# All stores of a grouped softmax move to SyncE's DMA ring, in turn with the loads

## The chip, the cores and the metric

The kernel runs on one core of one Trainium2 chip. Its time is device microseconds for one execution. Before the change it took 1326.51 us, the median of 4 runs that lie between 1326.36 and 1326.7 us. One further execution was taken with the hardware profiler on; the profile below is of that one.

The engines that matter here are VectorE (DVE in the profile), ScalarE (ACT), GpSimd (POOL) and SyncE (SP). All transfers between the chip's main memory and the on-chip buffers are made by the core's 16 DMA engines. An instruction stream that issues a transfer (SyncE's or GpSimd's) only puts work into a ring of its own on each of those 16 engines. TensorE does nothing in this kernel.

## The reference

The input x has the shape (4, 4096, 4352) in float32. Each row of 4352 numbers is cut into 8 groups of 544, and every group gets its own softmax:

```python
x_g = x.reshape(B, N, 8, 544)
x_g = x_g - x_g.max(axis=-1, keepdims=True)
exp = np.exp(x_g)
out = exp / exp.sum(axis=-1, keepdims=True)
```

There are 16,384 rows. 285.2 MB are read and 285.2 MB are written, and each number is used in only a handful of operations.

## The kernel before

A tile is 256 rows: 128 partitions with two rows each, so 8704 numbers (34,816 bytes) in every partition and 4352 KB in all. There are 64 tiles (`nt`), numbered from 0, and six buffers of that size (`NT = 6`, `bufs`). Tile t lives in buffer t modulo 6, and everything is done in place there.

For each tile the work is as follows.

- **Load.** SyncE issues one transfer for the whole tile (line 105). Only the last tile, 63, is loaded as two halves of one row per partition (line 108), so that its computation can begin half a tile earlier. Completion is counted on the semaphore `landed` of that buffer.
- **Maximum.** VectorE makes the negated maximum of the 16 groups of each partition in one instruction (`vector_max`, line 62). It waits for `landed`.
- **Exponential.** ScalarE makes 16 instructions, one for each group, which add the negated maximum, take exp and leave the group's sum (`scalar_exp`, line 86).
- **Scaling.** VectorE takes the reciprocal of the 16 sums (line 72) and multiplies the tile by it (line 75), which raises the semaphore `scaled` by one (`vector_scale`).
- **Store.** Tiles 0 to 61 are stored by GpSimd (line 118), one transfer each, counted on the semaphore `stored` of the buffer. The last two tiles (`LAST = 2`) are stored by SyncE (line 113).

VectorE's own order is written out at the end of the kernel: the maximum of tile n+1 comes ahead of the scaling of tile n. So the scaling of tile n stands behind the landing of tile n+1.

Two queues are set by hand. SyncE's queue holds the 64 loads in order; before the load of tile t, from tile 6 on, it waits until `stored` says that tile t-6 has left the buffer (line 102). After the last load come the last two stores, each behind its wait on `scaled`. GpSimd's queue holds 62 stores, each behind its wait on `scaled` (line 117), and then the final waits for everything that was stored. The two queues fill two different rings on each of the 16 DMA engines: loads are in the one, stores in the other.

Of the kernel before, what the change touches and what calls it, by code (L numbers as in the profile page):

```python
# [1 line left out]

# [4 lines left out]


@with_exitstack
def kernel(  # L10
    ctx: ExitStack,
    tc: tile.TileContext,
    x: bass.AP,
    out: bass.AP,
):
    nc = tc.nc
    G = 8
    P = 128
    R = 2
    NT = 6  # L20
    RG = R * G
    xf = x.flatten_outer_dims()
    of = out.flatten_outer_dims()
    N, D = xf.shape
    Dg = D // G
    nt = N // (P * R)
    LAST = 2
    FIRST = 2
    turns = (nt - 1 - FIRST) // NT
    f32 = mybir.dt.float32  # L30
    X = mybir.AxisListType.X
    Exp = mybir.ActivationFunctionType.Exp
    xt = xf.rearrange("(t p r) d -> t p (r d)", p=P, r=R)
    ot = of.rearrange("(t p r) d -> t p (r d)", p=P, r=R)

    landed = [tc.alloc_semaphore(f"landed{b}") for b in range(NT)]
    stored = [tc.alloc_semaphore(f"stored{b}") for b in range(NT)]
    last_landed = tc.alloc_semaphore("last_landed")
    last_stored = tc.alloc_semaphore("last_stored")


    max_done = tc.alloc_semaphore("max_done")
    exp_done = tc.alloc_semaphore("exp_done")
    rec_done = tc.alloc_semaphore("rec_done")
    scaled = tc.alloc_semaphore("scaled")

    ctx.enter_context(tc.tile_critical(  # L47
        sync_engine=mybir.EngineType.Pool, no_gpsimd_drain=True))
    bufs = [ctx.enter_context(nc.sbuf_tensor(f"xt{b}", [P, R * D], f32)) for b in range(NT)]
    mx = ctx.enter_context(nc.sbuf_tensor("mx", [P, NT, RG], f32))  # L50
    sm = ctx.enter_context(nc.sbuf_tensor("sm", [P, NT, RG], f32))
    rs = ctx.enter_context(nc.sbuf_tensor("rs", [P, NT, RG], f32))

    parts = [(t, slice(0, RG)) for t in range(nt - 1)]
    parts += [(nt - 1, slice(r * G, (r + 1) * G)) for r in range(R)]

    def groups(t, g):
        return bufs[t % NT][:, :].rearrange("p (g d) -> p g d", d=Dg)[:, g, :]

    def vector_max(n):  # L60
        t, g = parts[n]
        i = nc.vector.reduce_max(  # L62
            out=mx[:, t % NT, g], in_=groups(t, g), axis=X, negate=True)
        if g.start == 0:
            i.wait_op(landed[t % NT], 16 * (t // NT + 1), "sem-ge")
        else:
            i.wait_op(last_landed, 16, "sem-ge")
        i.then_inc(max_done, 1)

    def vector_scale(n):  # L70
        t, g = parts[n]
        nc.vector.reciprocal(out=rs[:, t % NT, g], in_=sm[:, t % NT, g]).wait_op(  # L72
            exp_done, n + 1, "sem-ge").then_inc(rec_done, 1)
        xg = groups(t, g)
        nc.vector.tensor_tensor(  # L75
            out=xg,
            in0=xg,
            in1=rs[:, t % NT, g].unsqueeze(2).to_broadcast([P, g.stop - g.start, Dg]),
            op=mybir.AluOpType.mult,
        ).wait_op(rec_done, n + 1, "sem-ge").then_inc(scaled, 1)  # L80

    def scalar_exp(n, count):
        t, gs = parts[n]
        xg = groups(t, gs)
        for g in range(gs.start, gs.stop):
            i = nc.scalar.activation(  # L86
                out=xg[:, g - gs.start, :],
                in_=xg[:, g - gs.start, :],
                func=Exp,
                bias=mx[:, t % NT, g:g + 1],  # L90
                scale=1.0,
                accum_out=sm[:, t % NT, g:g + 1],
            )
            if g == gs.start:
                i.wait_op(max_done, count, "sem-ge")
        i.then_inc(exp_done, 1)

    for t in range(nt):  # L100
        if t >= NT:
            nc.sync.wait_ge(stored[t % NT], 16 * (t // NT))
        tile_in = bufs[t % NT]
        if t < nt - 1:
            nc.sync.dma_start(out=tile_in[:, :], in_=xt[t]).then_inc(landed[t % NT], 16)  # L105
        else:
            for r in range(R):
                nc.sync.dma_start(
                    out=tile_in[:, r * D:(r + 1) * D], in_=xt[t, :, r * D:(r + 1) * D],
                ).then_inc(landed[t % NT] if r < R - 1 else last_landed, 16)  # L110
    for t in range(nt - LAST, nt):
        nc.sync.wait_ge(scaled, t + 1 if t < nt - 1 else len(parts))
        nc.sync.dma_start(out=ot[t], in_=bufs[t % NT][:, :]).then_inc(last_stored, 16)


    for t in range(nt - LAST):
        nc.gpsimd.wait_ge(scaled, t + 1)
        nc.gpsimd.dma_start(out=ot[t], in_=bufs[t % NT][:, :]).then_inc(stored[t % NT], 16)  # L118
    for t in range(nt - NT, nt - LAST):
        nc.gpsimd.wait_ge(stored[t % NT], 16 * (t // NT + 1))  # L120
    nc.gpsimd.drain()
    nc.gpsimd.wait_ge(last_stored, 16 * LAST)

    nc.scalar.preload_act_table(Exp)  # L124

    for n in range(FIRST):
        scalar_exp(n, n + 1)
    nc.scalar.sem_inc(max_done, -FIRST)
    with nc.scalar.Fori(0, turns):
        for k in range(NT):  # L130
            scalar_exp(FIRST + k, k + 1)
        nc.scalar.sem_inc(max_done, -NT)
    for k, n in enumerate(range(FIRST + turns * NT, len(parts))):
        scalar_exp(n, k + 1)


    vector_max(0)
    for n in range(len(parts)):
        if n + 1 < len(parts):
            vector_max(n + 1)  # L140
        vector_scale(n)


# [1 line left out]
_INS = ['x']  # L145
_OUTS = [((4, 4096, 4352), 'float32')]


# [23 lines left out]
```

## Time and profile before

| what | before |
|---|---|
| median of 4 runs | 1326.51 us (1326.36 to 1326.7) |
| the profiled execution, its own time | 1326.34 us |
| the profiled execution, its span from first to last instruction | 1324.6 us |
| VectorE busy | 1190.0 us (90%) |
| ScalarE busy | 757.4 us (57%) |
| GpSimd busy | 33.3 us (3%) |
| moved by DMA | 570.48 MB, mean 431 GB/s |

The page's first part gives the busy time of each engine. Its second part cuts the span in 40 equal slices and gives, for each, the busy share of the engines and of the 16 DMA engines (a 9 is 90% or more) and the rate at which these moved bytes. The third part tells apart the rings by their kind: the hardware kind is the one that SyncE's transfers fill, the software kind the one that GpSimd's fill, and the small third one brings instructions. The fifth part lists the costliest groups of instructions, each with its line, its count, its busy time in all, the mean of one, and the idle time of the engine just before them with what ended it. The sixth part lists the transfers with the time from issue to landing.

Of the execution's 1326.34 us, 1.7 us lie outside the span.

### The profile page before, as it was taken

The page shows a single profiled execution, that of the slowest core. Times are in us where ns is not written, and L with a number is a line of the kernel's source. Part 1 is how long each engine was busy: PE and PEld are TensorE (multiplying, and loading weights), DVE is VectorE, ACT ScalarE, POOL GpSimd, SP SyncE. Part 2 cuts the span into 40 slices and gives each one's busy share as a digit, 9 for nine tenths or more (in the row PEclk, how much of TensorE's full clock was granted, in tenths as well). Part 3 has the DMA queues.
Part 4 walks back from the last instruction along what each step waited for, and adds up shares of the span by engine and source line. Part 5 has one row for each costly group of instructions (what it writes and reads, how often), then busy time and mean ns, then how long its engine had stood idle before and what let it go on. Part 6 is the DMA issues. An engine that isn't in the chain of part 4 may idle for free.

```text
span 1324.6 us, 2465 instructions
## 1 busy us (share of the span) xinstructions
DVE 1190.0 (90%) x195; ACT 757.4 (57%) x2049; POOL 33.3 (3%) x66
## 2 busy tenths in 40 slices
DVE  5999999988989889898898998988989889898893
ACT  3765566547456465564655646556465474654751
POOL 0000000000000000000000000000000000000000
DMA  9999999999999999999999999999999999999998
GB/s 404 421 433 437 430 432 434 436 432 430 436 432 435 431 434 432 435 431 434 432 437 428 435 433 435 430 434 433 435 434 430 433 435 435 429 436 433 434 429 374
DMA packets 18582, 570.48 MB, mean 431 GB/s; under 512 B 2064, under 2 KB 2064, under 8 KB 2064
## 3 DMA queue, kind: packets, MB, share of 16 engines
q1 hardware_dynamic: 9648, 294.13, 51.5%
q0 software_dynamic: 8928, 276.30, 48.3%
q14 instruction: 6, 0.05, 0.0%
HBM read 285.21 MB, written 285.21 MB: 431 GB/s over the span
## 4 chain that ended last, share of the span: by engine, by line
another core or an unknown queue 69%; DVE 20%; DMA 7%; ACT 1%; SPq 1%; issue 0%; POOLq 0%
DVE xt L75 10%; DVE mx L62 10%; DMA out_dram<-xt 4%; DMA xt<-in_x_dram 3%; ACT xt L86 1%; SPq L105 1%; DVE rs L72 0%; SPq L167 0%; POOLq L47 0%; POOLq L156 0%
## 5 line engine op out<-in xcount | busy, mean ns | idle before, releaser
L86 ACT ACTIVATE xt<-xt,mx 128x544 f32<-128x544 f32 x1024 | 750.1, 734 | 542.4 <-DVE mx L62 542.4
L62 DVE TENSOR_REDUCE mx<-xt 128x16 f32<-128x8704 f32 (+1 forms) x65 | 590.1, 9079 | 110.7 <-DMA xt<-in_x_dram 110.7
L75 DVE TENSOR_TENSOR xt<-xt,rs 128x8704 f32<-128x8704 f32 (+1 forms) x65 | 590.6, 9086 | 2.2
L86 ACT ACTIVATION_READ_ACCUMULATOR xt<-xt,mx 128x1 f32 x1024 | 191.0, 186 | 0.0
L118 POOL DMA_DIRECT2D out_dram<-xt x62 | 33.1, 533 | 1243.4 <-DVE xt L75 1243.4
L72 DVE RECIPROCAL rs<-sm 128x16 f32<-128x16 f32 (+1 forms) x65 | 15.7, 242 | 2.8 <-ACT xt L86 2.8
L124 ACT ACT_TABLE_LOAD x1 | 1.3, 1283 | 0.9 <-PEq L156 0.9
L156 POOL MEMSET const-float32-0.0<- 128x1 f32 x1 | 0.1, 98 | 0.2 <-issue 0.2
L156 POOL MEMSET const-bfloat16-1.0<- 128x1 bf16 x1 | 0.1, 102 | 0.0
L156 POOL MEMSET const-float32-1.0<- 128x1 f32 x1 | 0.1, 98 | 0.0
L156 POOL MEMSET const-uint8-127<- 128x1 uint8 x1 | 0.1, 98 | 0.0
## 6 DMA issues: line engine op xcount, KB each, us to landing
xt<-in_x_dram SPq DMA_DIRECT2D x63, 4352.0 KB, 32.9
out_dram<-xt POOLq DMA_DIRECT2D x62, 4352.0 KB, 50.6
out_dram<-xt SPq DMA_DIRECT2D x2, 4352.0 KB, 20.1
xt<-in_x_dram SPq DMA_DIRECT2D x2, 2176.0 KB, 35.9
```

What stands on the lines that cost most here:

```text
L62: i = nc.vector.reduce_max(out=mx[:, t % NT, g], in_=groups(t, g), axis=X, negate=True)
L72: nc.vector.reciprocal(out=rs[:, t % NT, g], in_=sm[:, t % NT, g]).wait_op(exp_done, n + 1, "sem-ge").then_inc(rec_done, 1)
L75: nc.vector.tensor_tensor(out=xg, in0=xg, in1=rs[:, t % NT, g].unsqueeze(2).to_broadcast([P, g.stop - g.start, Dg]), op=mybir.AluOpType.mu ...
L86: i = nc.scalar.activation(out=xg[:, g - gs.start, :], in_=xg[:, g - gs.start, :], func=Exp, bias=mx[:, t % NT, g:g + 1], scale=1.0, accum ...
L105: nc.sync.dma_start(out=tile_in[:, :], in_=xt[t]).then_inc(landed[t % NT], 16)
L118: nc.gpsimd.dma_start(out=ot[t], in_=bufs[t % NT][:, :]).then_inc(stored[t % NT], 16)
L124: nc.scalar.preload_act_table(Exp)
L156: nc = _bacc.Bacc("TRN2", target_bir_lowering=False, num_devices=1)
```

## The change

GpSimd no longer issues any transfer. SyncE issues the six first loads, then store 0, then store 1, and from there on it goes in turn: after store i+1 is issued, SyncE waits until store i has landed and issues load i+6 into the buffer that this has made free. After load 63 (in two halves, as before) come the stores 59 to 63. Each store stands behind its wait on `scaled`, as it did on GpSimd. The last two stores still count on `last_stored`. GpSimd keeps only the final waits, and its drain goes. Tiles, buffers and all computation are as they were.

```diff
-    for t in range(nt):
-        if t >= NT:
-            nc.sync.wait_ge(stored[t % NT], 16 * (t // NT))
+    def load(t):
         tile_in = bufs[t % NT]
         if t < nt - 1:
             nc.sync.dma_start(out=tile_in[:, :], in_=xt[t]).then_inc(landed[t % NT], 16)
...
-    for t in range(nt - LAST, nt):
+
+    def store(t):
         nc.sync.wait_ge(scaled, t + 1 if t < nt - 1 else len(parts))
-        nc.sync.dma_start(out=ot[t], in_=bufs[t % NT][:, :]).then_inc(last_stored, 16)
+        nc.sync.dma_start(out=ot[t], in_=bufs[t % NT][:, :]).then_inc(
+            stored[t % NT] if t < nt - LAST else last_stored, 16)
 
+    for t in range(NT):
+        load(t)
+    for t in range(nt):
+        store(t)
+        if t >= 1 and t - 1 + NT < nt:
+            nc.sync.wait_ge(stored[(t - 1) % NT], 16 * ((t - 1) // NT + 1))
+            load(t - 1 + NT)
 
-    for t in range(nt - LAST):
-        nc.gpsimd.wait_ge(scaled, t + 1)
-        nc.gpsimd.dma_start(out=ot[t], in_=bufs[t % NT][:, :]).then_inc(stored[t % NT], 16)
     for t in range(nt - NT, nt - LAST):
         nc.gpsimd.wait_ge(stored[t % NT], 16 * (t // NT + 1))
-    nc.gpsimd.drain()
     nc.gpsimd.wait_ge(last_stored, 16 * LAST)
```

## The prediction

> **What bounds the kernel now.** I read the page's slices and DMA parts first, since the engines' shares (DVE 90%) could suggest a bound by VectorE.
>
> ```profile
> DMA  9999999999999999999999999999999999999998
> GB/s 404 421 433 437 430 432 434 436 432 430 436 432 435 431 434 432 435 431 434 432 437 428 435 433 435 430 434 433 435 434 430 433 435 435 429 436 433 434 429 374
> DMA packets 18582, 570.48 MB, mean 431 GB/s; under 512 B 2064, under 2 KB 2064, under 8 KB 2064
> q1 hardware_dynamic: 9648, 294.13, 51.5%
> q0 software_dynamic: 8928, 276.30, 48.3%
> ```
>
> The 16 DMA engines are busy from the first slice to the last, and the two rings share them to 99.8%. VectorE, in contrast, waits for loads:
>
> ```profile
> DVE mx L62 <- DMA xt<-in_x_dram: 110.7, 51, 13.8
> SPq L105 <- DMA out_dram<-xt: 1200.6, 57, 67.5
> ```
>
> These are lines of the list of waits (engine and line, what it waited for, us in all, times, longest). VectorE is late only because data is; SyncE waits 1200.6 us for stores to free a buffer. So the DMA engines set the pace.
>
> The question is then whether their pace depends on the mixture that they are given. The table by stretches answers it: from 16 to 44 us only loads are in flight, in one ring; from 300 to 1200 us loads and stores in two rings; from 1290 to 1319 us stores alone, in two rings and at the end in one.
>
> ```profile
> core 0: us, DVE busy (x) ACT busy (x) POOL busy (x), PEclk, DMA share, GB/s
> 16.00:44.00 28.00, 25.31 (x4) 20.99 (x57) 0.00 (x0) 1.00 1.00 432
> 300.00:1200.00 900.00, 812.35 (x131) 518.38 (x1406) 23.37 (x44) 1.00 1.00 433
> 1290.00:1319.00 29.00, 14.40 (x6) 5.96 (x16) 0.00 (x0) 1.00 1.01 437
> ```
>
> The last two columns are the DMA share and the rate: 432, 433 and 437 GB/s (the last is a short stretch, in which whole packets are counted by their start). Pure reading, a mixture turning from load to store with each packet, and pure writing all go at one rate. Read packet by packet, the trace says why: a packet is one partition's 34,816 bytes, its record lasts 1.288 us whatever it moves, and the next one on that engine starts 3 to 4 ns before its end, so one takes 1.2847 us. Between two transfers of one ring stands only the marker that raises the semaphore, which takes 6 ns. That holds in SyncE's ring from load to load at the start and from store 62 to store 63 at the end, where no other ring has work to fill a gap.
>
> The floor follows. A DMA engine has 570.48 MB / 16 = 35.65 MB at 34,816 bytes in 1.2847 us, which is 1315.6 us, and 129 markers of 6 ns, 0.8 us: 1316.4 us. The first packet starts 1.9 us into the span, and the last engine's last marker lands 1.9 us before its end. 1.9 + 1316.4 + 1.9 = 1320.2 of the span of 1324.6; so the latest engine loses 4.4 us in the whole run (the sixteen last markers lie between 1319.7 and 1322.7 us, so most engines lose about 2). Part of this can be seen:
>
> ```profile
> 44.00:47.00 3.00, 3.00 (x2) 2.53 (x8) 0.67 (x1) 1.00 1.01 418
> 47.00:50.00 3.00, 3.00 (x1) 0.00 (x0) 0.00 (x0) 1.00 0.96 302
> 50.00:53.00 3.00, 3.00 (x1) 0.00 (x0) 0.00 (x0) 1.00 0.94 406
> 53.00:56.00 3.00, 2.96 (x3) 2.47 (x7) 0.00 (x0) 1.00 0.97 418
> ```
>
> GpSimd issues its first store at 44.7 us. The rate over these 12 us is (418 + 302 + 406 + 418) / 4 = 386 instead of 433 GB/s: 12 x 47 / 433 = 1.3 us lost. I call this the dent. It comes once.
>
> **The change part by part.**
>
> *Removed from GpSimd:* 62 issues (line 118, 0.531 us each, 33 us in all), 62 waits and the drain. GpSimd's time is beside everything else, and its drain ends before the last store has landed: 0 us. The second ring goes with it.
>
> *Added to SyncE:* 62 issues at 0.343 to 0.348 us (its two present stores), 21 us in all, and 62 waits on `scaled`; the waits on `stored` are one for each of 58 loads, as before. It has 1200.6 us of waiting to hide the issues in: 0 us, so long as the ring never runs dry.
>
> *Does the ring run dry?* A load now stands behind two waits: that store i+1's tile is scaled, and that store i has landed. Behind these waits are all later loads and stores, and VectorE's maximum waits for the loads. The start is tightest. A transfer takes 8 x 1.2847 + 0.006 = 10.28 us. Load 0 lands at 13.7 us, load 5 five transfers later, at 65.1. Store 0 is scaled at 44.4 us and so is queued before that; it lands at 75.4. Store 1 (scaled at 62.9) runs until 85.7. Load 6 is issued at 75.4, when store 0 has landed, while store 1 still has 10.3 us to go; it runs until 96.0. Store 2 (scaled at 81.5) runs until 106.3, load 7 (issued at 85.7, with 10.3 us of load 6 and all of store 2 still to go) until 116.5, store 3 (scaled at 100.0) until 126.8. A store's margin, from scaled to its turn, is 20.7, 12.5, 14.5 and 16.5 us, and it grows by 2.0 with each tile, since two transfers take 20.56 us and VectorE's tile 18.55. Once VectorE waits for loads, it is 3 x 20.56 = 61.7 us from the landing of load t+1 to store t's turn, less 18.6 us for line 62 and line 75: 43 us. A load's margin is never below 10.3 us. The sixteen engines are spread by 3 us at the end and a landing and an issue take some 2 us (load 0: 1.0 us from issue to first packet, line 105 0.33 us); 5 us are left. No bubble: 0 us.
>
> *Does VectorE get its loads in time?* Load 6 lands at 96.0, and its maximum is due at 118.5. Loads then come each 20.56 us and VectorE needs one each 18.55 us, so it catches up after 11 tiles and from there waits for loads, as now. It is not on the path while the DMA engines are busy.
>
> *The end.* Behind load 62 the ring holds store 58, load 63, stores 59 to 63: 72 us. From the landing of load 62, VectorE needs its maximum (9.2), scaling 61 (9.4), the first half's maximum (4.7), scaling 62 (9.4), the second half's maximum (4.6), scaling the first half (4.9), then the second, which has to wait until 6.0 us of exponentials are done (1.2 + 4.9): 48 us. Store 63 has its turn after 62 us. Cover 14 us; 0 us. Before, the DMA engines were busy to the end as well, so there is no tail to gain.
>
> *The turn from one kind to the other inside one ring* is the one thing that no row shows. The order L0 to L5, S0, S1, L6, S2, L7 ... S58, L63, S59 has 59 turns from load to store and 58 back. From below: nothing can be gained at a turn, as packets of every mixture take 1.2847 us. From above: the dent, 1.3 us, if it is what the first store behind a load costs, at each of 59 turns. The nearer rows are the marker between two transfers of one ring (6 ns, load to load and store to store) and the turning from packet to packet, load to store, between two rings (no gap, 300 to 1200 us). I take 0 and keep 1.3 us for the range.
>
> *The dent:* with one ring nothing joins. If the dent belongs to the second ring, 1.3 us are won; if it belongs to the first writing, it comes again. I take half, -0.65.
>
> The Trainium skill has a rule that speaks against the change. Its page "DMA: Bandwidth & Descriptors", section "Anatomy of one DMA — SWDGE (gpsimd) path", gives each transfer a fixed cost of about 2.0 us, mostly the wait for the receipt of the last write. If a single ring left that open, 129 transfers would add 258 us; the same page, section "Two DMAs through the same engine are not ordered", says that descriptors of one queue start in order but are pipelined, by which it would add nothing. The 6 ns between transfers in the row above side with the second.
>
> **Sum.** 1326.34 - 0.65 + 0 = 1325.7 us against the profiled execution's own time. That one lies 0.17 us under the median of the runs, so 1325.9 us.
>
> **The rivals.** 0.2% is 2.65 us, about what a measurement of this kernel can tell from no change.
>
> - *Turns cost (slower).* At the dent's price: 59 x 1.3 = 77 us, 1403 us. It decides from 2.65 / 59 = 45 ns for each turn from load to store. For it: no stretch shows a store behind a load in one ring with nothing beside it. Against it: the equal rates of the three stretches.
> - *The ring runs dry (slower).* If scaled waits or landing times were 6 us worse than worked out, fast engines would idle in each round: 1 us in 58 rounds is 58 us, 1384 us. Against it: margins of 10 to 43 us.
> - *The stragglers go (faster).* If the losses of the latest engine come from the software ring, up to 4.4 us go: 1322 us. For it: the dent is on all engines, and the last marker trails the middle ones by some 2.5 us. Against it: instruction packets (six on q14, 0.3 us each) also push an engine back, and they stay.
>
> **How the numbers follow.** No change within 0.2%: 0.66. Turns cost: 0.21, with the ring running dry 0.25 for slower. Stragglers go by more than 2.65 us: 0.09. The likeliest case's own range is 1323.9 to 1327.5. The 8-in-10 range reaches to 1323.0 below, where 0.05 are left out, and above to 1334, which is a price of 0.14 us at 59 turns, a tenth of the dent; the 0.15 or so above it is the rest of the two slow cases.
>
> **What would show it.** Right: one ring with 18,576 packets and close to 100% of the span, 432 to 434 GB/s in all slices between the first and last, the dent at 44 to 56 us gone or moved to 65 us, SyncE waiting some 1200 us for stores, GpSimd without transfers. Turns cost: a rate below 430 GB/s throughout, with the DMA share below 1.00 or packets longer than 1.288 us. Ring dry: a share below 1.00 while VectorE's wait for loads grows, above all from 60 to 120 us. The prediction is wrong if mixed rings were what kept the engines fed.

## The result, and the profile after

The changed kernel takes 1329.72 us in the median of 50 runs (1328.06 to 1331.72), against 1326.49 us in the median of 75 runs of the kernel before (53 of them between 1326.28 and 1326.75, the others up to 1336.59). The ratio is 1.0021, with a 95% interval from 1.0017 to 1.0024: about 3 us slower, small but outside the noise. The forecast was 1325.9 us and no change.

The profiled execution took 1329.76 us with a span of 1328.0 us, 3.4 us more than the span before (1324.6 us). The parts of the page that carried the prediction now read as follows: slices and DMA rings first, then the list of waits.

```profile
DMA  9999999999999999999999999999999999999998
GB/s 403 424 431 434 431 434 427 429 435 430 434 430 430 433 435 433 434 431 432 434 436 432 433 431 433 434 436 431 434 430 433 436 434 432 432 432 433 434 434 346
DMA packets 18582, 570.48 MB, mean 430 GB/s; under 512 B 2064, under 2 KB 2064, under 8 KB 2064
q1 hardware_dynamic: 18576, 570.43, 99.7%
```

```profile
DVE mx L62 <- DMA xt<-in_x_dram: 107.4, 50, 13.7
SPq L103 <- DMA out_dram<-xt: 1069.3, 57, 20.7
SPq L112 <- DVE xt L75: 159.8, 13, 40.5
```

In the changed kernel's list of waits, line 103 issues loads and line 112 stores. One ring carries everything, the engines are busy in every slice, VectorE waits for loads as before, and SyncE has over 1000 us to spare. The ring did not run dry. Yet the mean rate is 430 instead of 431 GB/s, and the last slice is emptier (346 instead of 374).

The table by stretches says when time is lost. Of the kernel before (columns as in the prediction: VectorE, ScalarE and GpSimd busy, TensorE's clock, DMA share, GB/s):

```profile
80.00:300.00 220.00, 215.88 (x37) 135.29 (x368) 6.37 (x12) 1.00 1.00 433
300.00:600.00 300.00, 270.60 (x44) 175.79 (x478) 7.97 (x15) 1.00 1.00 433
600.00:1200.00 600.00, 541.75 (x88) 342.59 (x928) 15.40 (x29) 1.00 1.00 433
```

Of the changed kernel:

```profile
80.00:300.00 220.00, 219.01 (x37) 138.52 (x377) 0.00 (x0) 1.00 1.00 431
300.00:600.00 300.00, 269.17 (x44) 172.49 (x468) 0.00 (x0) 1.00 1.00 432
600.00:1200.00 600.00, 543.15 (x88) 342.61 (x928) 0.00 (x0) 1.00 1.00 433
```

The loss is early and stops: 431, then 432, then the old 433. The DMA share stays at 1.00, so engines are not idle; some packets take longer. And the end shows who pays. This is the DMA view from 1320 us to 1327 us, before:

```profile
DMA packets 14, 0.15 MB, mean 21 GB/s; under 512 B 9, under 2 KB 9, under 8 KB 9
q1 hardware_dynamic: 13, 0.14, 4.7%
```

and after:

```profile
DMA packets 32, 0.70 MB, mean 99 GB/s; under 512 B 12, under 2 KB 12, under 8 KB 12
q1 hardware_dynamic: 32, 0.70, 23.1%
```

Before, 0.15 MB were left to move at 1320 us; after, 0.70 MB are, by a few engines, while the others have finished at the old time. The sixteen last markers lie between 1319.7 and 1322.7 us before. After, nine lie between 1319.8 and 1320.2, and seven between 1322.6 and 1326.1 us. The latest one is 3.4 us later, and that is the whole difference between the two spans.

Since one ring takes the transfers in order, the markers of a transfer on the sixteen engines can be read off the trace one transfer after the other. Their distances from the first one show the late engines falling back:

```
changed kernel: distance of the 16 markers of one transfer from the first (us)
at   96 us  0.00 0.00 0.01 0.07 0.09 0.11 0.15 0.22 0.32 0.34 0.41 0.42 0.45 0.94 1.00 1.10
at  178 us  0.00 0.01 0.07 0.18 0.20 0.21 0.26 0.30 0.37 0.38 0.45 0.61 0.83 2.68 2.75 2.78
at  343 us  0.00 0.01 0.07 0.21 0.26 0.30 0.37 0.38 0.45 0.73 0.87 2.16 3.24 5.12 5.17 5.35
at  590 us  0.00 0.01 0.07 0.21 0.26 0.30 0.37 0.38 0.45 1.39 1.94 3.29 4.34 5.93 5.96 5.99
at 1248 us  0.00 0.01 0.07 0.21 0.26 0.30 0.37 0.38 0.45 2.79 3.29 3.51 4.35 5.93 5.96 5.99
```

The trace does not name the engine of a packet, but each can be followed from its end to the start of the next. Read in this way, the long packets after 80 us stand at one place: of 117 that exceed 1.31 us, at least 97 are the last or last but one packet of a load, directly ahead of a store in the ring. They are up to 0.75 us too long, 0.2 us in the median, most of them on engines that come to this turn later than the others, in most of the rounds (one store and one load) until about 450 us. Before, there is no such row. As a measure I take the *excess*: what the whole-size packets that start after 80 us took beyond 1.288 us, summed over the 16 engines. It is 4.6 us before and 30.2 us after, and about 25 of the 30.2 us stand at the last two packets of loads.

### The profile page after: what moved, and what is told of

The parts are those of the page before. It is cut to its first block, busy times and chain, and to the rows that moved or that the text cites. A ratio compares the mean times of both kernels' runs of the same rounds, so it can differ in the third digit from the quotient of the medians.

```text
span 1328.0 us, 2464 instructions
## 1 busy us (share of the span) xinstructions
DVE 1189.9 (90%) x195; ACT 757.4 (57%) x2049; POOL 0.2 (0%) x4
## 3 DMA queue, kind: packets, MB, share of 16 engines
q1 hardware_dynamic: 18576, 570.43, 99.7%
## 4 chain that ended last, share of the span: by engine, by line
DMA 80%; DVE 16%; ACT 1%; SPq 1%; issue 0%; POOLq 0%
DMA out_dram<-xt 77%; DVE xt L75 8%; DVE mx L62 8%; DMA xt<-in_x_dram 3%; ACT xt L86 1%; SPq L103 1%; DVE rs L72 0%; SPq L170 0%; POOLq L47 0%; POOLq L159 0%
```

## The experiments

The theory, A: with one ring, all engines have the same order of work and turn from loading to storing nearly together; an engine that comes a little late has its last load packets slowed, and falls back until the engines stand apart. With two rings each engine changes between load and store at every packet (in the kernel before, between 500 and 900 us, all 4150 successions that can be followed unambiguously do), so no crowd turns. The rivals: B, the addresses (the first 100 MB of the arrays turn more slowly); C, VectorE and ScalarE being busy at the turns in the early rounds; D, the kind of ring (stores from the hardware ring cost more than from the software ring). The ratios below are to runs of the kernel before that were taken beside each experiment, with medians of 1326.49 to 1326.51 us.

**One ring of the other kind.** The changed kernel with GpSimd issuing everything:

```diff
-            nc.sync.dma_start(out=tile_in[:, :], in_=xt[t]).then_inc(landed[t % NT], 16)
+            nc.gpsimd.dma_start(out=tile_in[:, :], in_=xt[t]).then_inc(landed[t % NT], 16)
...
-        nc.sync.dma_start(out=ot[t], in_=bufs[t % NT][:, :]).then_inc(
+        nc.gpsimd.dma_start(out=ot[t], in_=bufs[t % NT][:, :]).then_inc(
```

> The changed kernel's order (store i+1, then load i+6), but every transfer issued by GpSimd, so again one ring, of the software kind. Crowded turns (theory A: engines that share one order turn from load to store together, and some lose 0.1 to 1.0 us there): as the changed kernel, 1328 to 1332 us, late engines' last markers spread over 4 to 7 us. Ring kind (theory D: it is stores from the hardware ring that cost): as before, 1326 to 1327.5 us, markers spread by 3 us.

Measured: 1331.73 us, ratio 1.003 (1.0013 to 1.0048). The last markers lie between 1321.1 and 1327.1 us, and the excess is 35.9 us. A store in the software ring behind a load loses like one in the hardware ring: D is out.

**Two rings with the kinds exchanged.**

```diff
-            nc.sync.dma_start(out=tile_in[:, :], in_=xt[t]).then_inc(landed[t % NT], 16)
+            nc.gpsimd.dma_start(out=tile_in[:, :], in_=xt[t]).then_inc(landed[t % NT], 16)
...
-    for t in range(NT):
+    for t in range(nt):
+        if t >= NT:
+            nc.gpsimd.wait_ge(stored[t % NT], 16 * (t // NT))
         load(t)
     for t in range(nt):
         store(t)
-        if t >= 1 and t - 1 + NT < nt:
-            nc.sync.wait_ge(stored[(t - 1) % NT], 16 * ((t - 1) // NT + 1))
-            load(t - 1 + NT)
```

> Two rings as before the change, but with the kinds exchanged: all loads issued by GpSimd, all stores by SyncE. Theory A (crowded turns in one ring): as before, 1326 to 1327.5 us, and no packets beyond 1.31 us in a regular row after 80 us. Theory D (hardware stores cost): as the changed kernel, 1328 to 1332 us.

Measured: 1327.80 us, ratio 1.0003 (0.9981 to 1.0024). The excess is 5.2 us and the rate from 80 to 300 us is again 433 GB/s:

```profile
80.00:300.00 220.00, 215.10 (x35) 135.11 (x367) 5.80 (x11) 1.00 1.00 433
```

Two rings are free of the row of slow packets whichever kind carries the loads. The median is 0.3 us above the range expected; with the loads in the software ring, its first packet starts at 2.9 us instead of 1.9. The interval is too wide to tell this kernel from before or from the changed kernel by time alone; the excess decides.

**All engines together once more, in the middle.**

```diff
     for t in range(nt):
+        if t == nt // 2:
+            nc.sync.wait_ge(landed[(t + 4) % NT], 16 * ((t + 4) // NT + 1))
         store(t)
```

> The changed kernel, but SyncE waits once, before store 32, until load 36 has landed, so that the ring runs empty and all 16 engines start store 32 together. The bubble costs about 2 us. Theory A: the engines are close together again, so the slow last packets of loads come back after store 32 for some 10 to 20 turns, and the latest engine loses another 3 to 5 us: 1334 to 1338 us. Theory B (addresses: the first 100 MB of the arrays are slower to turn on) and theory C (VectorE being busy at the turn in the first rounds): nothing new after store 32, 1331 to 1333 us.

Measured: 1337.69 us, ratio 1.0064 (1.0041 to 1.0087), inside A's range. This is the strongest single test. The stretches of the profiled execution, which took 1336.01 us and was the fastest of ten:

```profile
600.00:700.00 100.00, 90.21 (x16) 59.07 (x160) 0.00 (x0) 1.00 1.00 434
700.00:760.00 60.00, 52.33 (x9) 32.54 (x89) 0.00 (x0) 1.00 0.94 392
760.00:900.00 140.00, 122.91 (x22) 75.37 (x205) 0.00 (x0) 1.00 1.00 427
900.00:1100.00 200.00, 179.21 (x29) 116.56 (x316) 0.00 (x0) 1.00 1.00 432
```

Before the pause the kernel runs at 434 GB/s. The pause falls between 700 and 760 us (store 32 begins 25.4 us after store 31 instead of 20.6). After it the rate is 427 GB/s for 140 us, with the engines at a share of 1.00, and then climbs back. The excess from 760 to 900 us is 32.0 us, where the changed kernel has 0.3 us. The addresses from there on are far beyond the first 100 MB, and VectorE waits for loads: B and C both forecast nothing here. Directly after the pause every one of the 16 engines loses: the last packet of store 32 on each took 12.0 us too long in sum, the last two of load 37 18.1 us. From the next load on the loss is smaller. So with all engines in step, packets of a store ahead of a load are slowed as well.

**The computation cut.**

```diff
-            out=mx[:, t % NT, g], in_=groups(t, g), axis=X, negate=True)
+            out=mx[:, t % NT, g], in_=groups(t, g)[:, :, 0:8], axis=X, negate=True)
...
-        xg = groups(t, g)
+        xg = groups(t, g)[:, :, 0:8]
...
-                out=xg[:, g - gs.start, :],
-                in_=xg[:, g - gs.start, :],
+                out=xg[:, g - gs.start, 0:8],
+                in_=xg[:, g - gs.start, 0:8],
```

> The changed kernel with its transfers untouched and its computation cut: maximum, exp and scaling touch 8 numbers of each group of 544, the rest is stored as it was loaded. Theory C (VectorE and ScalarE at work beside the turns slow them): the slow packets go, 1326 to 1327 us. Theories A and B: they stay, 1328 to 1332 us.

Measured: 1330.61 us, ratio 1.0023 (1.0005 to 1.004). VectorE is busy for 7.37 of the 220 us and the rate is as low as with the full computation:

```profile
80.00:300.00 220.00, 7.37 (x30) 46.45 (x320) 0.00 (x0) 1.00 1.00 430
```

The excess is 38.5 us, about 30 of it at the last two packets of loads. C is out.

**Half as many turns.** Two stores, then two loads:

```diff
-    for t in range(nt):
-        store(t)
-        if t >= 1 and t - 1 + NT < nt:
-            nc.sync.wait_ge(stored[(t - 1) % NT], 16 * ((t - 1) // NT + 1))
-            load(t - 1 + NT)
+    for t in range(0, nt, 2):
+        store(t)
+        store(t + 1)
+        for b in (t, t + 1):
+            if b + NT < nt:
+                nc.sync.wait_ge(stored[b % NT], 16 * (b // NT + 1))
+                load(b + NT)
```

> One ring as in the changed kernel, but in turn by twos: stores i and i+1, then loads i+6 and i+7. The turns from load to store fall from 59 to 30. Theory A in the form 'each close turn costs the late engines something until they stand apart': fewer close turns, but the same spread to reach, so between before and after, 1327 to 1329.5 us, with the excess of packet time from 80 us on below the 27 to 34 us (summed over 16 engines) of the one-ring kernels. If only the final spread counts: 1329 to 1330.5 us. If the spread has nothing to do with the number of turns but the loss does: about half of the changed kernel's extra 3.2 us, 1328 us.

Measured: 1330.66 us, ratio 1.0023 (1.0013 to 1.0034): no less than with 59 turns. The excess is 37.0 us, and it goes on longer, with 5.8 us of it still from 900 to 1200 us. The last markers lie between 1320.1 and 1327.3 us. So the loss is not a price for each turn; it is nearest to the form in which only the final spread counts (1329 to 1330.5 us).

**Twice as many turns.**

```diff
+    def store(t, r):
+        c = slice(r * D, (r + 1) * D)
...
+        for r in range(R):
+            store(t, r)
+            if t >= 1 and t - 1 + NT < nt:
+                nc.sync.wait_ge((stored, stored1)[r][(t - 1) % NT], 16 * ((t - 1) // NT + 1))
+                load(t - 1 + NT, r)
```

> The changed kernel with each tile loaded and stored as two halves (one row per partition each), in turn half by half: 117 turns from load to store, packets of 17,408 bytes. The 128 further markers cost 128 x 6 ns = 0.8 us. Theory A with a loss in proportion to the number of turns: 1329.7 + 0.8 + 3 = 1333 to 1335 us. Theory A with a loss that ends once the engines stand apart: 1329 to 1332 us.

Measured: 1334.02 us, ratio 1.0047 (1.0033 to 1.0061). By its size this looks like the loss in proportion to the turns, but the trace says otherwise, because my floor was wrong. Two packets of 17,408 bytes take 2 x 644.6 ns, 4.5 ns more than one of 34,816 bytes; for 1016 such pairs on an engine that is 4.6 us, and with 0.8 us of markers the floor is 5.4 us higher. The first eleven engines end between 1325.0 and 1325.4 us, 5.2 us later than the first nine of the changed kernel. The latest engine is 5.6 us behind the first, where in the changed kernel it was 6.4. The spread has not grown with the turns.

**No writing of main memory: all loads.** The stores 0 to 61 are loads of the same tile instead:

```diff
-        nc.sync.dma_start(out=ot[t], in_=bufs[t % NT][:, :]).then_inc(
+        nc.sync.dma_start(
+            out=bufs[t % NT][:, :] if t < nt - LAST else ot[t],
+            in_=xt[t] if t < nt - LAST else bufs[t % NT][:, :],
+        ).then_inc(
```

> The changed kernel with all its waits and its order, but the stores 0 to 61 are replaced by loads of the same tile into the same buffer (so only the last two tiles are written). Nothing turns from reading to writing memory. If the slow packets belong to the turn of kind: none in a regular row, also no dent at the first of the replaced stores, 1324.5 to 1326 us. If they belong to the waits, the markers or the issuing in turn: as the changed kernel, 1328 to 1332 us.

Measured: 1328.95 us, ratio 1.0011 (1.0 to 1.0023), so the time is between the two forecasts. The packets decide part of it. The regular row of slow packets is gone: 5 packets after 80 us are longer than 1.31 us, against 117 in the changed kernel. The loss at the first turn is gone too: the excess from 60 to 80 us is 0.9 us, against 12.1. So waits, markers and issuing in turn are not the cause by themselves. But all packets have become longer by some 4 ns, on every engine and for the whole run, which the forecast did not have. All but three of the last markers lie between 1322.7 and 1323.4 us; the latest is at 1325.1.

**No writing of main memory: copies of a buffer onto itself.** The same place, with `in_=bufs[t % NT][:, :]` for the stores 0 to 61:

> The changed kernel with all waits and its order, but the stores 0 to 61 are replaced by copies of the buffer onto itself, so that a turn still goes from writing a buffer to reading one but main memory is not written before tile 62. If the slow last packets need the writing of main memory: none in a regular row, no dent from 60 to 80 us (such packets may take another time of their own, so the whole is not to be compared with 1326 us). If reading a buffer after loads is what costs: slow last packets of loads and a dent of 10 to 13 us summed over the engines, as in the changed kernel.

Measured: 1329.58 us, ratio 1.0022 (1.0012 to 1.0032). The time is not to be compared; again all packets are longer by some 4 ns. The regular row is gone here as well, with 9 packets over 1.31 us after 80 us. But the excess from 60 to 80 us is 9.6 us, nearly as large as in the changed kernel. So there are two effects. The regular row of slow packets needs the writing of main memory. The loss at the very first turn does not; here it came where buffers are first read behind loads, and with loads alone it was 0.9 us.

Where this first loss stands can be read off the packets. In the changed kernel they start between 60 and 64 us, so they are the last packets of load 5, ahead of store 0. The rates are of the changed kernel, and the second stretch shows the gap that the long packets leave:

```profile
60.00:64.00 4.00, 4.00 (x2) 4.00 (x13) 0.00 (x0) 1.00 1.16 418
64.00:68.00 4.00, 4.00 (x1) 1.32 (x4) 0.00 (x0) 1.00 0.87 374
```

In the kernel before, the long packets, from 46.4 us on, are all in the ring of the loads; the first packets of store 0 start at 49.65 us and take 1.288 us. That a buffer is read for the first time is neither needed nor enough. The run with the pause has such a loss on all engines in the middle (tiles 32 and 37), in buffers read many times before, and the two kernels that follow have none at their first store.

**Eight engines set back from the start.**

```diff
+    for j in range(4):
+        nc.sync.dma_start(out=bufs[NT - 1][16 * j:16 * j + 8, :], in_=xt[NT - 1, 16 * j:16 * j + 8, :]).then_inc(spread[j], 16)
     for t in range(NT):
+        if t == NT - 1:
+            for j in range(4):
+                nc.sync.wait_ge(spread[j], 16)
         load(t)
```

> The changed kernel, with 4 small loads ahead of load 0 (8 partitions each, one packet for each of 8 DMA engines, into rows of buffer 5 that load 5 overwrites later). They put 8 engines 4 x 1.285 = 5.1 us behind the other 8 from the start. Theory A: with half as many engines turning together, the excess of packet time from 80 us on falls well below that of the changed kernel (27 to 34 us summed over 16 engines), to 5 to 15 us; the time is the late group's, 1326.5 + 5.1 - 2.6 to 1326.5 + 5.1, so 1329 to 1332 us. If standing apart does not help: the late group loses 3 us more and the excess stays, 1333 to 1336 us.

Measured: 1344.19 us, ratio 1.0121 (1.0095 to 1.0147), far outside both ranges. The small loads are the reason: all packets that start in the first 16 us, theirs and the first of load 0, took 3.2 to 4.9 us instead of 1.3, and the first slice of this run falls to 232 GB/s. That loss is at the start, before any turn. What the run was made for it shows clearly. From 80 us on, the rate is that of two rings:

```profile
80.00:300.00 220.00, 219.59 (x37) 139.19 (x378) 0.00 (x0) 1.00 1.00 433
```

The excess is 4.1 us, less than before the change. The first store follows load 5 at 78.4 us here, and the excess from 76 to 100 us is 0.3 us: there is no loss at the first turn. The early eight engines keep their places, and five of the late eight; the other three fall back by up to some 2 us over the run:

```
8 engines set back: distance of the 16 markers of one transfer from the first (us)
at   89 us  0.00 0.03 0.05 0.05 0.07 0.08 0.08 0.15 4.26 4.31 4.36 4.36 4.40 4.43 4.59 5.16
at  664 us  0.00 0.03 0.05 0.05 0.07 0.08 0.08 0.15 4.31 4.36 4.36 4.43 4.59 4.97 5.69 5.80
at 1158 us  0.00 0.03 0.05 0.05 0.07 0.08 0.08 0.15 4.32 4.36 4.36 4.43 4.59 4.97 5.80 7.02
```

The late eight end spread over 3.0 us, as the sixteen do in the kernel before. One ring, 59 turns from load to store, all stores to main memory, and no loss beyond that of two rings, with only half of the engines turning together.

**Four engines set back.** The same with 4 partitions in each small load.

> As the kernel with 8 engines set back, but the 4 small loads have 4 partitions each, so 4 engines are set back and 12 stay together. Theory A in the form 'up to about 8 or 9 engines turn together without a loss, more do not' (the changed kernel ended with 9 together, the kernel with two groups of 8 lost nothing): some of the 12 lose, an excess of packet time from 80 us on of 8 to 20 us summed over the engines, and a dent from 60 to 80 us of some us. If any gap between two groups is enough: an excess below 5 us and no dent.

Measured: 1346.20 us, ratio 1.015 (1.0133 to 1.0167), again with the costly start. The excess after 80 us is 16.6 us, in the forecast range, but not on the engines I had named. Eleven stay together and lose at most 0.4 us each; their last markers lie between 1332.1 and 1332.5 us. The five others, from 1.8 to 6.1 us behind at 98 us, fall back slowly for the whole run, to between 7.1 and 9.3 us. The dent that I expected is not there: the first store begins at 77.5 us, and the excess from 76 to 100 us is 0.2 us.

Taken together: a late engine's last load packets are slowed when most of the others (9 of 16 in the changed kernel, 11 here) have turned to storing already; when half have (8 and 8), hardly any are. Where all 16 stand together, at the first turn and after the pause, all of them lose. That the row of slow packets needs engines turning as a crowd is shown from both sides: it goes with two rings and with eight engines set back, and it comes back when a pause puts all engines in step. That it needs the writing of main memory is shown by the two kernels that hardly write, with the reserve that all their packets differ by 4 ns. What in the memory or the path to it holds up those packets is not shown. Why later turns cost less than the first is open. So is why six of the seven late engines of the changed kernel nearly stop falling back, at anything from 1.9 to 6 us (the seventh drifts on slowly); in the kernel with four set back, engines still lose at 5 to 8 us.

## Why the prediction was wrong, point by point

- *The bound* was right. The DMA engines are busy to 99.7%, and VectorE and SyncE wait as forecast.
- *The ring does not run dry* and *the end is covered*: right. SyncE's issues found their margin, and the share is 1.00 in all stretches between 80 and 1200 us.
- *The turn inside one ring, taken at 0*: this is the step that failed. In place of 0, late engines lost up to some 5 us each, nearly all of it at the last packets of loads, and the latest one ended 3.4 us later than the latest before. I had weighed the marker between transfers of one kind (6 ns) and the turning from packet to packet between two rings. Neither row shows engines turning as a crowd: in the stretch of loads alone and in that of stores alone all engines do the same for its whole length, and in the mixture each engine changes at every packet, at a moment of its own.
- *The rival "turns cost"* had the place and the sign right and the form wrong. It priced each turn alike, on all engines, for 59 turns (1403 us). The price was paid by seven engines, mostly in the first 20 rounds, and neither halving nor doubling the turns changed the final spread much (7.2 and 5.6 us, against 6.4). Its sign, packets longer than 1.288 us, did show; the rate stayed at 431 GB/s or more in the stretches from 80 us on and the DMA share at 1.00.
- *The dent, half of 1.3 us won*: wrong. By the packets the dent was 0.9 us an engine, not 1.3: the excess from 44 to 60 us before was 15.0 us over the 16 engines. After, it is 0.3 there, and 12.1 us from 60 to 80 us, at the end of load 5. So it belongs neither to the second ring nor, as the copies of a buffer onto itself showed, to the first writing. It came again almost whole: 0.2 us for each engine were won instead of 0.65.
- *The stragglers go*: the opposite. I had put the 4.4 us of the latest engine down as something that a single ring could only lessen.
- *The page's fixed cost*: the Trainium skill's 2.0 us for each transfer ("DMA: Bandwidth & Descriptors", section "Anatomy of one DMA — SWDGE (gpsimd) path") did not appear between queued transfers of one ring here, nor with all transfers in GpSimd's ring (1331.73 us); 129 of them would have been 258 us, and the whole change was 3.2.

- *The range* of 1323.0 to 1334 us holds the measured time, because it left room above for a price of 0.14 us at each of 59 turns. That is luck in part: the size fell into the room, but the loss is no price for each turn.

The latest engine's last marker, 3.4 us later with the dent and the turns both in it, gives 1326.34 + 3.4 = 1329.7 us, against 1329.76 us in the profiled execution.

## What to carry to other kernels

When the DMA engines are the bound, equal mean rates in stretches of loads, of stores and of both do not say what an order of transfers will cost: ask what all 16 engines do at the same moment, and look at the spread of the last markers and not only at the mean rate, since the latest engine sets the end. Two rings, one with loads and one with stores, mix the directions at each packet and keep the engines from turning as a crowd; one ring gave that up here for 0.2%, and no order in one ring that was tried won it back. Forcing all engines into step in the middle of a stream cost more here than the pause itself: the span grew by 6.2 us, for a pause that put store 32 off by 4.8 us.

## What was not expected of the hardware

- Kernels that hardly write main memory had packets longer by some 4 ns throughout (all loads: 1328.95 us in all), though a stretch of loads alone at the start of the kernel before ran at 432 GB/s. Why is open.
- Splitting packets in two costs 4.5 ns for each pair, 4.6 us in this kernel.
- At the start of the kernel with eight engines set back, four small loads into 8 neighbouring partitions each, and the packets of load 0 beside them, took 3.2 to 4.9 us for each packet of 34,816 bytes. In the kernel before, the first packets of load 0 took 1.3 to 2.4 us and later ones 1.288 us. Why is open.
